# Input projection of a Mamba-2 layer in pairs of tiles: seven half-size products instead of eight

## The chip, the core and the metric

The kernel runs on one core of a Trainium2 chip. The core has five engines with an instruction queue each: TensorE (PE, matrix products, with its weight loads shown as PEld), VectorE (DVE, element-wise work), ScalarE (ACT, element-wise functions), GpSimd (POOL) and SyncE (SP), which here issues the DMA transfers. An engine works through its own queue in order and waits on semaphores for the others. [...] The metric is the device time of one execution in microseconds.

## What is computed

One layer (DEPTH is 1): RMSNorm, an input projection, a causal convolution, a state-space scan, a gate, RMSNorm, an output projection, the residual, and a last RMSNorm. x is 512 tokens of 2048 features.

```python
def ssm_mixer(h, w_in, conv_w, conv_b, dt_bias, a_log, d_skip, norm_g, w_out):
    proj = h @ w_in                                  # (512, 2048) @ (2048, 10304)
    z = proj[..., :D_INNER]                          # 4096
    xbc = proj[..., D_INNER:D_INNER + CONV_DIM]      # 4096 of x, 1024 of B, 1024 of C
    dt = proj[..., D_INNER + CONV_DIM:]              # 64
    xbc = jax.nn.silu(causal_depthwise_conv(xbc, conv_w, conv_b)).astype(jnp.float32)
    ...
    y = ssd_chunked_scan(xs * dt[..., None], dt * a, bm, cm)
    y = y + d_skip.astype(jnp.float32).reshape(g, r, 1) * xs
    y = y.reshape(bsz, length, D_INNER) * jax.nn.silu(z.astype(jnp.float32))
    y = rmsnorm(y, norm_g)
    return y.astype(h.dtype) @ w_out
```

All is f32. The product `h @ w_in` is 80 column tiles of 128 (32 of x, 32 of z, 8 of B, 8 of C) and dt.

## The kernel before

**Products in three terms.** TensorE works on the type fp32r. Each operand is split into a high part (ScalarE's cast, L80) and a low part (VectorE's subtraction, L81), and a product is hi·hi + hi·lo + lo·hi: three matmuls (`mm_k`, L177 to L179). A weight *piece* is half a column tile, 128x1024 f32 (eight blocks of 128 features). `load_piece` (L74) fetches it on SP's queue, `split_piece` splits it; the buffers `raw` (2) and `hi`, `lo` (3 each) go round. The normalised x lies split in `xh`, `xl`, one 128x512 tile for each of the 16 blocks of features.

**Order.** `seq` lists 80 column tiles: B0, C0, then for each unit u the tiles x_u and z_u; ahead of each second unit of a group of four stand the next group's B and C. A tile is 16 steps (blocks of features) of three matmuls with 512 columns into one PSUM tile `mm`, 48 matmuls in all. At its end `finish` hands it to `conv_silu` (x, B, C: scaling into `xr`, L361, four convolution steps L363 and L366, Silu L368) or to `u_z` (gate).

**State-space work.** A unit is two heads. Its steps hang on step numbers in a table `ev`: `u_load` fetches rows of decay exponents (`csb`, `ecs`), `u_decay` makes the masked decay matrix `m` (L436 to L444) with the group's `cbm` (L409), `u_xt` transposes x (L456), `u_state` (L477), `u_yd` (L489, L493), `u_yo` (L380 to L382, L511 to L520), which stores y to DRAM. TensorE and SP run in the order in which the program is written; VectorE and ScalarE are ordered by the framework's scheduler when the kernel is built, and keep that order on the chip.

**Behind it** come the output projection (`mm_o`, L629 to L631, from 1002.8 us on) and the last norm. The change leaves their arithmetic alone.

Of the kernel before, what the change touches and what calls it, by code (L numbers as in the profile page):

```python
# [28 lines left out]
EPS = 1e-6  # L29


@with_exitstack
def mamba_layer(ctx: ExitStack, tc: tile.TileContext, d: dict, out: bass.AP):
# [7 lines left out]
    yp0 = ctx.enter_context(tc.tile_pool(name="yp0", bufs=1))  # L41
# [30 lines left out]
    def load_piece(src, shape):  # L72
        raw = wp.tile(shape, F32, name="raw", bufs=2)
        nc.sync.dma_start(raw, src)  # L74
        return raw

    def split_piece(raw, shape, pool):
        hi = pool.tile(shape, F32R, name="hi")
        lo = pool.tile(shape, F32R, name="lo")
        S.copy(out=hi, in_=raw)  # L80
        V.tensor_tensor(out=lo, in0=raw, in1=hi, op=ALU.subtract)  # L81
        return hi, lo
# [35 lines left out]
    NP = 2 * len(seq)  # L118
    pieces = {}

    def w_src(n):
        kind, i = seq[n // 2]
        return d["wi"][tile_of[kind] + i, :, (n % 2) * 8:(n % 2) * 8 + 8, :]

    def get_piece(n):
        if n in pieces or n >= NP + len(wo_order):
            return
        if n < NP:
            pieces[n] = split_piece(load_piece(w_src(n), WSH), WSH, wp)
        else:  # L130
            p, s = wo_order[n - NP]
            pieces[n] = split_piece(load_piece(wo_src(p, s), OSH), OSH, op if n % 4 == 3 else wp)


    xh = [xp.tile([P, L], F32R, name=f"xh{k}") for k in range(KT)]
    xl = [xp.tile([P, L], F32R, name=f"xl{k}") for k in range(KT)]
    xr = sp.tile([P, L + 3], F32, name="xr")

    xbuf = [("csb", 2), ("csb", 2), ("m", 2), ("msh", 1), ("msl", 1)]

    def load_x(k2):
        name, bufs = xbuf[k2 % 5]
        raw = sp.tile([P, 2, L], F32, name=name, bufs=bufs)
        n = 2 if k2 else 1
        for j in range(0, 2, n):
            nc.sync.dma_start(raw[:, j:j + n, :], d["xT"][:, 2 * k2 + j:2 * k2 + j + n, :])
        return raw

    def split_x(k2, raw):
        for j in range(2):  # L150
            k = 2 * k2 + j
            S.activation(xh[k], raw[:, j, :], AF.Identity, scale=lng[:, k:k + 1])
            V.scalar_tensor_tensor(out=xl[k], in0=raw[:, j, :], scalar=lng[:, k:k + 1],
                                   in1=xh[k].bitcast(F32), op0=ALU.mult, op1=ALU.subtract)
# [20 lines left out]
    def mm_k(ps, w, k8, k):  # L175
        hi, lo = w
        T.matmul(ps, hi[:, k8, :], xh[k], start=k == 0, stop=False)  # L177
        T.matmul(ps, hi[:, k8, :], xl[k], start=False, stop=False)  # L178
        T.matmul(ps, lo[:, k8, :], xh[k], start=False, stop=k == KT - 1)  # L179
# [28 lines left out]
    for k in range(KT):  # L208
# [35 lines left out]
        for t in range(2):  # L244
            mm_k(ps_bc[:, t, :], w0[t, k // 8], k % 8, k)
# [6 lines left out]
    for i in (0, 2):  # L252
# [81 lines left out]
    def dt_sums():  # L334
# [5 lines left out]
        V.tensor_tensor(out=nwl, in0=cs, in1=pl, op=ALU.subtract)  # L340
        V.tensor_tensor(out=win[:, 0, :], in0=nwl[:, 0, :], in1=pl[:, 1, :], op=ALU.subtract)
        V.tensor_copy(out=win[:, 1, :], in_=nwl[:, 1, :])
        S.activation(win, win, AF.Exp, scale=-1.0)

    def dt_spread():
# [3 lines left out]
        cst = sp.tile([H, NC, P], F32, name="xd", bufs=2)  # L349
# [9 lines left out]
    def conv_silu(ps, t, name, bufs):  # L359

        V.tensor_tensor(out=xr[:, 3:L + 3], in0=ps, in1=rbc, op=ALU.mult)  # L361
        ca = sp.tile([P, L], F32, name=name, bufs=bufs)
# [7 lines left out]

    def split(src, shape, name, bufs=1):
# [6 lines left out]
    def mm3(o, a, b, sa, sb):  # L378

        T.matmul(o, a[0][sa], b[0][sb], start=True, stop=False)  # L380
# [31 lines left out]
    def u_load(u):  # L412
        csb = sp.tile([P, 2, L], F32, name="csb", bufs=2)
# [6 lines left out]
    def u_decay(u):  # L420
# [3 lines left out]
        m = sp.tile([P, 2, 6 * P], F32, name="m", bufs=2)  # L424
        ma = m[:, :, 0:4 * P].rearrange("p c (h l) -> p c h l", h=2)
        mb = m[:, :, 4 * P:6 * P].rearrange("p c (h l) -> p c h l", h=2)
        for i in range(2):
            for hh in range(2):
# [3 lines left out]
                for o, l, b in ((ma[:, i, hh, 0:P], la, cs[:, 2 * i, h:h + 1]),  # L432
                                (ma[:, i, hh, P:2 * P], lb, nwl[:, 2 * i, h:h + 1]),
                                (mb[:, i, hh, :], lb, cs[:, 2 * i + 1, h:h + 1])):
                    if i == 0:
                        S.activation(o, l, AF.Relu, scale=-1.0, bias=b)  # L436
                    else:
# [320 lines left out]
```

## Time and profile before

| | |
|---|---|
| median of 3 runs | 1374.59 us (1374.23 to 1374.94) |
| profiled execution | 1374.24 us, of which the span of the trace is 1372.5 |
| granted TensorE clock, mean | 0.997 |
| TensorE busy, 0 to 115 us / 115 to 1002.8 / behind | 107.4 / 887.8 / 360.5 us |
| VectorE busy in these stretches | 89.3 / 568.3 / 219.0 us |
| ScalarE busy in these stretches | 71.0 / 442.2 / 113.5 us |

A row of the trace's timeline has the start in us, the length in us, the engine, the line of the kernel, the operation, what it writes and reads, the shapes, and in brackets how long the engine had stood idle and who ended that. A row of the groups ends with busy time and mean length in ns, then the idle time before and its releasers. A row of the stretches has the stretch, its length, and the busy time and number of instructions of each engine, the granted clock, the share of the DMA engines and GB/s. In a row of the chain, engines stand with their share of the span.

### The profile page before, as it was taken

The numbers are of one execution on the slowest core, as the hardware profiler recorded it, in microseconds if no ns is written. First come the engines' busy times: TensorE is split into PE (matmuls) and PEld (weight loads), VectorE is DVE, ScalarE is ACT, GpSimd is POOL, SyncE is SP. The second block draws the span as 40 slices with busy tenths as digits, with TensorE's granted clock in tenths as the row PEclk, the third lists the DMA queues.
The fourth block names the chain that finished last, engine by engine and source line by source line (L and its number), as shares of the span: only waits on it lengthen the run. The fifth ranks groups of instructions, "written<-read, shape, count | busy, mean of one in ns | idle before, by whom it ended". The sixth has DMA issues, their size and how long they took to land.

```text
span 1372.5 us, 16466 instructions
## 1 busy us (share of the span) xinstructions
PE 1355.7 (99%) x6388; PEld 1097.1 (80%) x6388; DVE 876.7 (64%) x1433; ACT 626.6 (46%) x894; POOL 1.7 (0%) x11
## 2 busy tenths in 40 slices
PE   7999999999999999999999999999999999999997
PEld 5888878888888888888878888888888888888885
DVE  7867665765666575666557665667647665566545
ACT  7455653635465273546346443736453222223213
POOL 0000000000000000000000000000000000000000
PEclk9999999999999999999999999999999999999998
DMA  7333443523433252434324343424444445454402
GB/s 235 94 113 104 146 126 98 160 58 131 130 112 115 77 158 87 150 100 133 107 77 161 97 134 102 147 92 131 128 146 145 146 152 169 146 163 147 137 30 93
DMA packets 55182, 170.85 MB, mean 124 GB/s; under 512 B 6720, under 2 KB 11136, under 8 KB 54976
## 3 DMA queue, kind: packets, MB, share of 16 engines
q1 hardware_dynamic: 54384, 167.95, 38.4%
q10 hardware_dynamic: 720, 1.84, 0.4%
q8 instruction: 50, 0.82, 0.2%
q14 instruction: 28, 0.23, 0.1%
HBM read 156.99 MB, written 12.78 MB: 124 GB/s over the span
## 4 chain that ended last, share of the span: by engine, by line
PE 97%; DMA 1%; DVE 0%; SPq 0%; ACT 0%; issue 0%; DVEq 0%; ACTq 0%
PE mm L177 21%; PE mm L179 21%; PE mm L178 21%; PE mm L630 9%; PE mm L629 9%; PE mm L631 9%; PE yd L489 2%; DMA raw<-in_wi 1%; PE yd L493 1%; PE tr L456 1%; PE st L477 1%; PE yo L381 0%; PE yo L380 0%; PE yo L382 0%; PE tr L299 0%; PE tr L381 0%
## 5 line engine op out<-in xcount | busy, mean ns | idle before, releaser
L177 PE MATMUL mm<-xh,hi 128*128 128x512 f32 x1248 | 497.1, 398 | 0.0
L179 PE MATMUL mm<-xh,lo 128*128 128x512 f32 x1248 | 489.0, 392 | 0.0
L178 PE MATMUL mm<-xl,hi 128*128 128x512 f32 x1248 | 488.6, 392 | 0.0
L81 DVE TENSOR_TENSOR lo<-raw,hi 128x1024 fp32r<-128x1024 f32 x212 | 258.8, 1221 | 151.8 <-ACT hi L80 151.6
L80 ACT CAST hi<-raw 128x1024 fp32r<-128x1024 f32 x212 | 220.9, 1045 | 262.9 <-PE mm L178 108.6
L179 PEld LDWEIGHTS mm<-xh,lo 128*128 128x128 f32 x1248 | 234.4, 188 | 52.5
L177 PEld LDWEIGHTS mm<-xh,hi 128*128 128x128 f32 x1248 | 234.6, 188 | 51.7 <-issue 5.3
L178 PEld LDWEIGHTS mm<-xl,hi 128*128 128x128 f32 x1248 | 234.7, 188 | 46.2
L630 PE MATMUL mm<-lo,yh 128*128 128x512 f32 x512 | 201.9, 394 | 0.0
L629 PE MATMUL mm<-hi,yh 128*128 128x512 f32 x512 | 201.7, 394 | 0.0
L631 PE MATMUL mm<-hi,yl 128*128 128x512 f32 x512 | 201.7, 394 | 0.0
L629 PEld LDWEIGHTS mm<-hi,yh 128*128 128x128 f32 x512 | 96.2, 188 | 23.2 <-ACT acc L682 0.6
L631 PEld LDWEIGHTS mm<-hi,yl 128*128 128x128 f32 x512 | 96.1, 188 | 22.4
L630 PEld LDWEIGHTS mm<-lo,yh 128*128 128x128 f32 x512 | 96.1, 188 | 22.2
L519 ACT ACTIVATE z<-y 128x512 f32<-128x512 f32 x31 | 19.6, 633 | 123.5 <-DVE y L513 123.5
L686 DVE SCALAR_TENSOR_TENSOR acc<-mm,ry,acc 128x512 f32<-128x512 f32 x72 | 53.4, 747 | 30.5 <-PE mm L631 29.6
L366 DVE SCALAR_TENSOR_TENSOR xs<-xr,par,xs 128x512 f32<-128x512 f32 x96 | 71.8, 748 | 1.4
L436 ACT ACTIVATE m<-csb,cs 128x128 f32<-128x128 f32 x128 | 47.1, 391 | 51.4 <-DMA csb<-cscr 38.1
L442 DVE TENSOR_TENSOR m<-m,cbm 128x512 f32<-128x512 f32 x64 | 44.1, 689 | 38.5 <-ACT m L439 24.2
L368 ACT ACTIVATE xs<-xs 128x512 f32<-128x512 f32 x32 | 20.2, 632 | 69.2 <-DVE xs L366 69.2
L438 DVE TENSOR_SCALAR m<-csb,cs 128x128 f32<-128x128 f32 x128 | 33.7, 280 | 24.5 <-DMA csb<-cscr 24.4
L458 DVE TENSOR_TENSOR xd<-tr,dt 128x512 f32<-128x512 f32 x32 | 22.0, 687 | 31.3 <-PE tr L456 31.3
(211 smaller groups left out, 1173.2 us busy)
## 6 DMA issues: line engine op xcount, KB each, us to landing
raw<-in_wi SPq DMA_DIRECT2D x158, 512.0 KB, 3.9
raw<-in_wo SPq DMA_DIRECT2D x64, 512.0 KB, 4.1
csb<-cscr SPq DMA_DIRECT2D x32, 512.0 KB, 5.8
yscr<-y SPq DMA_DIRECT2D x32, 256.0 KB, 2.3
yr<-yscr SPq DMA_DIRECT2D x16, 512.0 KB, 4.7
ecs<-escr SPq DMA_DIRECT2D x64, 64.0 KB, 5.4
xt<-in_x SPq DMA_DIRECT2D x16, 256.0 KB, 4.6
csb<-in_xT SPq DMA_DIRECT2D x3, 512.0 KB, 8.9
```

Of the source, the lines that this page charges most:

```text
L80: S.copy(out=hi, in_=raw)
L81: V.tensor_tensor(out=lo, in0=raw, in1=hi, op=ALU.subtract)
L177: T.matmul(ps, hi[:, k8, :], xh[k], start=k == 0, stop=False)
L178: T.matmul(ps, hi[:, k8, :], xl[k], start=False, stop=False)
L179: T.matmul(ps, lo[:, k8, :], xh[k], start=False, stop=k == KT - 1)
L366: V.scalar_tensor_tensor(out=ca, in0=xr[:, k:k + L], scalar=convw[:, t, k:k + 1], in1=ca, op0=ALU.mult, op1=ALU.add)
L436: S.activation(o, l, AF.Relu, scale=-1.0, bias=b)
L442: V.tensor_tensor(out=ma[:, i], in0=ma[:, i], op=ALU.mult, in1=cbm[:, i, 0:2, :].rearrange("p b l -> p (b l)").unsqueeze(1).to_broadcast([ ...
L629: T.matmul(ps, yh, hi, start=k == 0, stop=False)
L630: T.matmul(ps, yh, lo, start=False, stop=False)
L631: T.matmul(ps, yl, hi, start=False, stop=k == n - 1)
L686: V.scalar_tensor_tensor(out=a, in0=ps, scalar=ry[:, t:t + 1], in1=a, op0=ALU.mult, op1=ALU.add)
```

## The change

The first four pairs of tiles (B0 C0, x0 z0, x1 z1, B1 C1: `plain`) are computed as before. The other 36 pairs (`quads`) are computed by a scheme of seven products of half size. Call the pair's first tile (x or B) p and its second (z or C) q. The features are cut in two halves, the tokens too. The four weight pieces of a pair are R11 and R12 (p's two halves of features) and R21, R22 (q's), and sums of them serve as operands too:

- T1 = R11 + R12, T2 = T1 + R22, T3 = R12 + R22, T4 = T2 + R21: four sums by VectorE, in place (`q_add`, L561), each then split like a piece: seven splits a pair.
- The other operands are halves of x and sums of them (`x_forms`, in `form`, and `x_form3`, which overwrites a quarter of `xh`, `xl`), made once and kept on chip.
- Each product is 8 blocks x 3 matmuls of 256 columns. They run in the order R11, T4 *of the pair before*, T1, R21, T2, R22, T3. R11, T2 and T3 add up in one half of a PSUM tile S (even pairs the one half, odd pairs the other), T1 and R22 in R; R21 and T4 in the `mm` tile of p. ScalarE copies S into that `mm` tile after R11 and after T3 (L603, L615), S and R into `sn` after T2 and T1 (L610, L607); VectorE adds them up to q (L612, L614).
- 28 steps (of six matmuls) a pair in the step table instead of 32 of three.

Beside it: the split products of B with C and of the state become f32 products (L408, L409, L462); the decay is made by ScalarE alone with one VectorE product of 128x1536 (L436); `csb`, `m` and `xd` have one buffer instead of two; R11's split has a buffer of its own, `h1h`, `h1l`; units' steps come later (`ramp` and the six numbers behind it); the wider PSUM for the output projection opens 1.5 blocks later.

```diff
-MANUAL = {mybir.EngineType.PE, mybir.EngineType.SP}
+MANUAL = {mybir.EngineType.PE, mybir.EngineType.SP, mybir.EngineType.Pool}
...
+    plain = [s for pair in (seq[0], seq[1], seq[2], seq[3]) for s in pair]
+    quads = seq[NPL // 2:]
+    QS = 28
...
+    def x_forms(g, j):
+        k = 4 * g + 2 * j
...
+        V.tensor_tensor(out=t1, in0=n2[:, :, hi_], in1=n1[:, :, hi_], op=ALU.subtract)
+        V.scalar_tensor_tensor(out=t2, in0=t1, scalar=-1.0, in1=n1[:, :, lo_], op0=ALU.mult, op1=ALU.subtract)
+        put(1, t1)
+        V.scalar_tensor_tensor(out=t1, in0=t2, scalar=-1.0, in1=n2[:, :, lo_], op0=ALU.mult, op1=ALU.subtract)
+        put(2, t2)
+        put(4, t1)
...
+    def q_add(n, f, old, other):
+        raw = qs[n][old]
+        V.tensor_tensor(out=raw, in0=raw, in1=qs[n][other], op=ALU.add)
+        qs[n][f] = raw
...
+    def q_events(n):
+        b = NPL * KT + n * QS
+        for o, f, a in ((-34, q_load, ("R11", 0, 0, "ra")), (-9, q_split, ("R11", True)),
+                        (-7, q_load, ("R12", 0, 1, "rb")), (-1, q_add, ("T1", "R11", "R12")),
+                        (0, q_split, ("T1",)), (-5, q_load, ("R21", 1, 0, "rc")), (2, q_split, ("R21",)),
+                        (-4, q_load, ("R22", 1, 1, "rc")), (10, q_add, ("T2", "T1", "R22")),
+                        (11, q_split, ("T2",)), (16, q_split, ("R22",)), (17, q_add, ("T3", "R12", "R22")),
+                        (18, q_split, ("T3",)), (21, q_add, ("T4", "T2", "R21")), (22, q_split, ("T4",))):
+            add(b + o, f, n, *a)
...
+    def product(ps, w, f, first, step):
+        for k in range(KH):
+            if k % 2 == 0:
+                run(step + k // 2)
+            hi, lo = w()
+            ah, al = operand(f, k)
+            T.matmul(ps, hi[:, k, :], ah, start=first and k == 0, stop=False, skip_group_check=True)
+            T.matmul(ps, hi[:, k, :], al, start=False, stop=False, skip_group_check=True)
+            T.matmul(ps, lo[:, k, :], ah, start=False, stop=k == KH - 1, skip_group_check=True)
+
+    def pair(n, prev):
...
+        s_, r_ = [x[:, (n % 2) * LH:(n % 2) * LH + LH] for x in SR]
...
+        product(s_, W("R11"), 11, True, b)
+        S.copy(out=A[:, lo_], in_=s_)
+        if prev:
+            prev(b + 4)
+        product(r_, W("T1"), 1, True, b + 8)
+        S.copy(out=sn[:, 1, :], in_=r_)
+        product(A[:, lo_], W("R21"), 12, False, b + 12)
+        product(s_, W("T2"), 2, False, b + 16)
+        S.copy(out=sn[:, 0, :], in_=s_)
+        product(r_, W("R22"), 4, False, b + 20)
+        V.tensor_tensor(out=zq[:, lo_], in0=r_, in1=sn[:, 0, :], op=ALU.add)
+        product(s_, W("T3"), 3, False, b + 24)
+        V.tensor_tensor(out=zq[:, hi_], in0=s_, in1=sn[:, 1, :], op=ALU.add)
+        S.copy(out=A[:, hi_], in_=s_)
...
+        def last(step):
+            product(A[:, hi_], W("T4"), 22, False, step)
+            normed(A)
+            (g_b if kp == "B" else u_x)(ip)
...
+        w = ramp[u] if u < len(ramp) else [24, 38, 50, 58, 61, 66]
+        for o, f in zip(w, (u_load, u_decay, u_xt, u_state, u_yd, u_yo)):
+            add(at["x", u] + o, f, u)
...
+    for i in range(4):
+        add(49 + 7 * i, x_forms, i // 2, i % 2)
+        add(120 + 2 * i, x_form3, i)
```

**What moves on VectorE, in the middle of the run.** Before, VectorE's queue from the scaling of a finished x tile (`xr`) on; the weight piece that is split between (`lo<-raw`) is one that TensorE needs two pieces later.

```order
L361 TENSOR_TENSOR xr<-mm,rbc 128x512 [waits DVE_49,PE_49]
L438 TENSOR_SCALAR m<-csb,nwl 128x128
L363 TENSOR_SCALAR xs<-xr,par 128x512 [waits DVE_49]
L81 TENSOR_TENSOR lo<-raw,hi 128x1024 [waits DMAHW0_49,Activation_49]
L366 SCALAR_TENSOR_TENSOR xs<-xr,par,xs 128x512 [waits DVE_49]
L438 TENSOR_SCALAR m<-csb,cs 128x128
```

Now, in the third pair of a group: T3's sum (`rb<-rb,rc`), `xr` when T4 of the pair before is done, the convolution with the steps behind `yo` between, `m`, the running sum of squares, and then T2's low part (`lo<-ra,hi`).

```order
L561 TENSOR_TENSOR rb<-rb,rc 128x1024
L374 TENSOR_TENSOR xr<-mm,rbc 128x512 [waits PE_49]
L365 TENSOR_SCALAR xs<-xr,par 128x512 [waits DVE_49]
L492 TENSOR_TENSOR ecs<-yo,ecs 128x256 [waits DMAHW6_49,DMAHW5_49,PE_49]
L368 SCALAR_TENSOR_TENSOR xs<-xr,par,xs 128x512 [waits DVE_49]
L493 TENSOR_TENSOR y<-y,ecs 128x256 [waits DVE_49]
L368 SCALAR_TENSOR_TENSOR xs<-xr,par,xs 128x512 [waits DVE_49]
L494 TENSOR_TENSOR y<-y,z 128x512 [waits DVE_49]
L368 SCALAR_TENSOR_TENSOR xs<-xr,par,xs 128x512 [waits DVE_49]
L436 TENSOR_TENSOR m<-m,cbm 128x1536 [waits Activation_49]
L500 TENSOR_TENSOR sx<-sx,z 128x512 [waits Activation_49]
L82 TENSOR_TENSOR lo<-ra,hi 128x1024
```

T2 is the third product behind T4 on TensorE, so its split stands behind work that begins only with T4's end. In the same place T1, R22 and T3 stand ahead of or behind this run of rows.

**What moves on TensorE where one piece of work follows another.** Before, the last matmuls of one column tile and the first of the next: they write different PSUM tiles (`mm_3755`, `mm_3869`) and wait for nothing.

```order
L178 MATMUL mm_3755<-xl15_137,hi_3707 128x512
L179 MATMUL mm_3755<-xh15_121,lo_3708 128x512
L177 MATMUL mm_3869<-xh0_106,hi_3751 128x512
L178 MATMUL mm_3869<-xl0_122,hi_3751 128x512
L179 MATMUL mm_3869<-xh0_106,lo_3752 128x512
```

Now, the last matmuls of T3 and the first of the next pair's R11, both into S:

```order
L590 MATMUL S<-xl,hi 128x256
L591 MATMUL S<-xh,lo 128x256
L589 MATMUL S<-xh,h1h 128x256 [waits Activation_49]
L590 MATMUL S<-xl,h1h 128x256
L591 MATMUL S<-xh,h1l 128x256
```

The wait is new. The count that it waits for is that of ScalarE's copy of S into `mm` (L615), which stands on ScalarE's queue thus, and itself waits for VectorE's read of S (L614):

```order
L610 COPY sn<-S 128x256 [waits PE_49]
L81 CAST hi<-ra 128x1024 [waits DVE_49,PE_49,Activation_49]
L615 COPY mm<-S 128x256 [waits DVE_49]
L621 ACTIVATE z<-z 128x512 [waits DVE_49]
L81 CAST hi<-rc 128x1024 [waits DMAHW3_49,PE_49,Activation_49]
```

What moved: a read of PSUM that ran beside the next tile's matmuls now stands between two products of TensorE.

More of the change, by code (lines that the diff above doesn't have):

```diff
@@ L286, in dt_load @@
     def dt_load():
-        wd = load_piece(d["wdt"], [P, KT, HD])
-        wa = [sp.tile([P, KT // 2, P], F32R, name=n) for n in ("msh", "msl")]
+        wd = load_piece(d["wdt"], [P, KT, HD], "rb")
+        wa = [sp.tile([P, KT // 2, P], F32R, name=n) for n in ("csb", "m")]
         for i in range(2):
@@ L369, in conv_silu, with normed @@
         return ca
+    def normed(ps):
+        V.tensor_tensor(out=xr[:, 3:L + 3], in0=ps, in1=rbc, op=ALU.mult)
     def split(src, shape, name, bufs=1):
@@ L518, in u_yo, with put @@
         else:
-            S.activation(sq, y, AF.Square)
-            V.tensor_tensor(out=sx, in0=sx, in1=sq, op=ALU.add)
+            S.activation(z, y, AF.Square)
+            V.tensor_tensor(out=sx, in0=sx, in1=z, op=ALU.add)
+    lo_, hi_ = slice(0, LH), slice(LH, L)
+    form = {}
+    def x_forms(g, j):
+        k = 4 * g + 2 * j
+        n1, n2 = [(sp if n in ("csb", "m") else wp).tile([P, 2, L], F32, name=n, bufs=1)
+                  for n in (("csb", "m"), ("h1h", "h1l"))[j]]
+        for n, k0 in ((n1, k), (n2, KH + k)):
+            nc.sync.dma_start(n, d["xT"][:, k0:k0 + 2, :])
+            for i in range(2):
+                S.activation(n[:, i, :], n[:, i, :], AF.Identity, scale=lng[:, k0 + i:k0 + i + 1])
+        if j == 0:
+            for f, s in ((1, 0), (2, 4), (4, 8)):
+                form[f, g] = [xp.tile(SSH, F32R, name=f"s{s + 2 * g + i}") for i in range(2)]
+        jj = slice(2 * j, 2 * j + 2)
+        t = wp.tile([P, 2, 2, LH], F32, name="rc", bufs=2)
+        t1, t2 = t[:, 0], t[:, 1]
+        def put(f, t):
+            hi, lo = [x[:, jj, :] for x in form[f, g]]
+            S.copy(out=hi, in_=t)
+            V.tensor_tensor(out=lo, in0=t, in1=hi, op=ALU.subtract)
+        V.tensor_tensor(out=t1, in0=n2[:, :, hi_], in1=n1[:, :, hi_], op=ALU.subtract)
[4 more added lines that the diff above has]
+        put(4, t1)
@@ new lines, in x_form3, with q_split @@
+    def x_form3(j):
+        kk = slice(2 * j, 2 * j + 2)
+        h, lo = xh[:, kk, hi_], xl[:, kk, hi_]
+        t = sp.tile([P, 2, LH], F32, name="y", bufs=2)
+        V.tensor_tensor(out=t, in0=xh[:, kk, lo_], in1=h, op=ALU.subtract)
+        V.tensor_tensor(out=t, in0=t, in1=xl[:, kk, lo_], op=ALU.add)
+        V.tensor_tensor(out=t, in0=t, in1=lo, op=ALU.subtract)
+        S.copy(out=h, in_=t)
+        V.tensor_tensor(out=lo, in0=t, in1=h, op=ALU.subtract)
+    def q_split(n, f, own=False):
+        raw = qs[n][f]
+        qs[n, f] = split_piece(raw, WSH, wp, *((("h1h", "h1l"), 1) if own else ()))
@@ L598, in mamba_layer @@
     add(b0 + 56, dt_spread)
-    for n in range(2, len(seq)):
+    for n in range(2, NPL):
         ps = None
@@ L614, in mamba_layer @@
             finish(n, ps)
+    prev = None
+    SR = [ps_q.tile([P, L], F32, name=x) for x in ("S", "R")]
+    for n in range(len(quads)):
+        prev = pair(n, prev)
+    prev(END)
     phx.close()
-    assert NP + 3 not in pieces
     op = ctx.enter_context(tc.tile_pool(name="op", bufs=1, side="right"))
     acc = [op.tile([P, DM], F32, name=f"acc{t}") for t in range(NC)]
-    step = len(seq) * KT
+    step = END + 4
     def mm_o(ps, blk, w, t):
```

302 lines of the change are left out of this document (151 added, 151 removed).

## The prediction

> **What bounds the kernel now.** I read the page's totals first, then its chain of work, then the busy time of the engines over the stretch that the change rewrites. That stretch runs from the end of the eighth column tile (115 us) to the first matmul of the output projection (1002.8 us).
>
> ```profile
> span 1372.5 us, 16466 instructions
> PE 1355.7 (99%) x6388; PEld 1097.1 (80%) x6388; DVE 876.7 (64%) x1433; ACT 626.6 (46%) x894; POOL 1.7 (0%) x11
> PE 97%; DMA 1%; DVE 0%; SPq 0%; ACT 0%; issue 0%; DVEq 0%; ACTq 0%
> 115.00:1002.80 887.80, 887.80 (x4333) 720.25 (x4332) 568.31 (x968) 442.15 (x628) 0.00 (x0) 1.00 0.37 116
> ```
>
> The reader is to see that TensorE (PE) has no idle time at all in these 887.8 us, that VectorE (DVE) is busy for 64% of them and ScalarE (ACT) for half. The 36 pairs of tiles take 887.8/36 = 24.66 us each: 96 matmuls and the state-space work between them. VectorE waits, never TensorE.
>
> **Durations that the sum uses.** On TensorE the listed length of a matmul holds its latency, so I take distances between starts: two rows twelve matmuls apart for 512 columns, and a burst of six with 256 columns, each with weights of its own (the only such burst), up to the matmul behind it.
>
> ```profile
> 399.66 0.39 PE L177 MATMUL mm<-xh,hi 128*128 128x512 f32 x1
> 402.40 0.39 PE L177 MATMUL mm<-xh,hi 128*128 128x512 f32 x1
> ```
> ```profile
> 1006.95 0.28 PE L477 MATMUL st<-xwsh,bth 128*128 128x256 f32 x1
> 1006.95 0.19 PEld L477 LDWEIGHTS st<-xwsl,bth 128*128 128x128 f32 x1
> 1007.54 0.28 PE L477 MATMUL st<-xwsh,btl 128*128 128x256 f32 x1
> 1007.66 0.39 PE L629 MATMUL mm<-hi,yh 128*128 128x512 f32 x1
> ```
>
> 512 columns: 2.74/12 = 0.228 us. 256 columns: 0.71/6 = 0.118 us, a little over half. The listed 0.19 us of a weight load overlap the matmul ahead, so it sets no pace in the burst. After a wait it is seen:
>
> ```profile
> 14.63 1.41 DVE L153 SCALAR_TENSOR_TENSOR xl<-m,lng,xh 128x512 fp32r<-128x512 f32 x2
> 15.44 0.50 PE L178 MATMUL yd<-xl,hi 128*128 128x512 f32 x1 [0.63 <-DVE xl L153]
> 15.78 0.40 PE L179 MATMUL yd<-xh,lo 128*128 128x512 f32 x1
> ```
>
> The first of these two operations of VectorE ends at 15.38 and TensorE starts 0.06 us later; its matmul takes 0.34 instead of 0.23 up to the next. A wait thus costs 0.06 + 0.11 = 0.17 us more.
>
> ```profile
> 638.45 0.65 PE L489 MATMUL yd<-m,xd 128*64 128x256 f32 x4
> 639.90 0.51 PE L177 MATMUL mm<-xh,hi 128*128 128x512 f32 x1
> ```
> ```profile
> L336 PE MATMUL tr<-y,mask 128*128 128x256 f32 x2 | 0.6, 378 | 0.0
> L380 PE MATMUL yo<-csth,stsh 128*128 128x256 f32 x32 | 9.0, 280 | 0.0
> ```
>
> The matmuls of one unit's `yd` occupy 1.45 us. A full-width f32 pass of 256 columns is listed 98 ns longer than the 256-column form above, so it streams for 118 + 98 = 216 ns. The new f32 state (two matmuls, each of two passes over 128 columns) is then about 0.45 us, the new f32 `cbm` products 4 x 0.216 + 4 x 0.108 = 1.3 us a group. These two are estimates. A unit's four transposes I set at 0.5 us, its three `yo` matmuls at 0.35.
>
> ```profile
> 612.72 1.22 DVE L81 TENSOR_TENSOR lo<-raw,hi 128x1024 fp32r<-128x1024 f32 x1
> 613.85 0.74 DVE L366 SCALAR_TENSOR_TENSOR bc<-xr,par,bc 128x512 f32<-128x512 f32 x1
> 614.51 1.22 DVE L81 TENSOR_TENSOR lo<-raw,hi 128x1024 fp32r<-128x1024 f32 x1
> 616.31 0.42 DVE L444 TENSOR_TENSOR m<-m,cbm 128x256 f32<-128x256 f32 x1
> 616.65 0.68 DVE L442 TENSOR_TENSOR m<-m,cbm 128x512 f32<-128x512 f32 x1
> 622.47 0.69 DVE L361 TENSOR_TENSOR xr<-mm,rbc 128x512 f32<-128x512 f32 x1
> 623.07 0.28 DVE L438 TENSOR_SCALAR m<-csb,nwl 128x128 f32<-128x128 f32 x1
> 623.26 0.54 DVE L363 TENSOR_SCALAR xs<-xr,par 128x512 f32<-128x512 f32 x1
> 623.72 1.22 DVE L81 TENSOR_TENSOR lo<-raw,hi 128x1024 fp32r<-128x1024 f32 x1
> ```
> ```profile
> 48.29 0.69 DVE L361 TENSOR_TENSOR xr<-yd,rbc 128x512 f32<-128x512 f32 x1
> 49.02 0.55 DVE L363 TENSOR_SCALAR bc<-xr,par 128x512 f32<-128x512 f32 x1
> ```
>
> VectorE back to back: 1.13 us for 128x1024 of two tensors, 0.60 for 512, 0.34 for 256, 0.66 for the three-operand form of 512, 0.46 for the one-tensor form. This is a base of 0.07 us and 1.04 ns an element, so the new `m` product of 1536 is 1.67. A result that the next instruction needs costs 0.13 more (0.73 instead of 0.60).
>
> ```profile
> L80 ACT CAST hi<-raw 128x1024 fp32r<-128x1024 f32 x212 | 220.9, 1045 | 262.9 <-PE mm L178 108.6 <-PE mm L631 92.8 <-DMA raw<-in_wi 34.6
> L374 ACT CAST stsh<-st 128x256 fp32r<-128x256 f32 x16 | 5.9, 371 | 50.0 <-PE st L477 50.0
> ```
> ```profile
> 607.38 0.40 ACT L436 ACTIVATE m<-csb,cs 128x128 f32<-128x128 f32 x1 [0.46 <-DMA csb<-cscr]
> 607.69 0.39 ACT L436 ACTIVATE m<-csb,nwl 128x128 f32<-128x128 f32 x1
> 609.27 1.28 ACT L439 ACT_TABLE_LOAD   x1
> ```
> ```profile
> 605.60 1.05 ACT L80 CAST hi<-raw 128x1024 fp32r<-128x1024 f32 x1 [0.46 <-DMA raw<-in_wi]
> 606.68 1.23 DVE L81 TENSOR_TENSOR lo<-raw,hi 128x1024 fp32r<-128x1024 f32 x1 [0.82 <-ACT hi L80]
> ```
> ```profile
> 77.77 0.39 PE L177 MATMUL mm<-xh,hi 128*128 128x512 f32 x1
> 77.97 0.69 DVE L361 TENSOR_TENSOR xr<-mm,rbc 128x512 f32<-128x512 f32 x1 [1.92 <-PE mm L179]
> ```
>
> ScalarE casts 128x1024 in 1.05 us and copies 256 columns out of PSUM in 0.37; a decay step of 128 takes 0.31, a change of its function table 1.28. From ScalarE's end to VectorE's start pass 0.03 us, and from the moment TensorE is free for its next matmul to the reader of its result 0.20.
>
> **The change, part by part.** *Matmuls:* 96 x 0.228 = 21.9 us a pair become 168 x 0.118 = 19.9. With 2.75 us of unit work a pair would take 22.6 us if TensorE never waited, 2 us less than now. *VectorE:* seven splits 7.9 us and four sums 4.5 (now four splits, 4.5), sums out of PSUM 0.7, z, xr and xd 1.8, convolution 2.4, `m` 1.67, xw and the state's split 0.5, y 0.66, the chain behind `yo` 1.9: 22.1 us a unit pair. It fits under 22.6 only if it is never late.
>
> *The loop.* It is late, because of two orders shown above. First, the product R11 of a pair writes the same PSUM tile S from which the last product of the pair before (T3) is still to be read, and TensorE waits there for ScalarE's copy, which itself waits for VectorE's read. Second, T2's low part stands on VectorE behind the whole convolution of the x tile, which can only begin when T4 is done. Followed from the end of one T3 (time 0) to the end of the next:
> - read of S at 0.20, 0.42 us; 0.03; copy 0.37; 0.17: R11 starts at **1.2**.
> - R11 24 x 0.118 = 2.84 and the state 0.45: done 4.5. T4 and `yd`, 2.84 + 1.5, end at 8.8.
> - `h1h` has one buffer: the cast of the next R11 waits for R11's end, 0.20 + 1.05 + 0.03, so VectorE begins its low part at 5.8. Behind it stand T2's sum, y and T3's sum: 1.13 + 1.13 + 0.66 + 1.13. VectorE reaches `xr` at **9.8**, so T4's end is no longer what it waits for.
> - `xr` 0.60, dependent 0.13, 0.46, ecs 0.34, three of 0.66, 0.34, 0.60, `m` 1.67, sum of squares 0.60, T2's low part 1.22: 7.9. It is ready at **17.8**. TensorE reached T2 at 1.2 + 4 x 2.84 + 0.45 + 1.5 + 0.35 = 14.9 and waits for some 2.6 us behind two matmuls that need only the high part.
> - from there 0.17, 22 x 0.118 = 2.6 to T2's end, R22 with transposes 3.34, T3 2.84, in all 8.95: **26.7**.
>
> Against 24.66 that is 2.0 us more. The five pairs of a group differ: the first (unit 4g) has the `cbm` products too, 28.0. In the second the sum of squares stands behind T2's low part, but ScalarE's cast for R21 stands ahead of the copy of S and delays R11 by about 1 us: `xr` at 2.2 + 7.7 + 0.2 = 10.1, then 7.3 and 8.95, 26.4. The third (B and C) 26.7. In the fourth T2's low part stands directly behind `xr`, so that only the wait for the copy is left: 1.2 + 19.9 + 2.5 = 23.6. In the fifth VectorE comes 0.9 us late to S and ScalarE begins the decay only at 7.5, after two casts that wait for R11; it takes 12 x 0.31 + 1.28 + 0.95 = 5.9. At 13.4 follow `m`, a convolution step and T2's low part, 1.67 + 0.66 + 1.22: 16.95, and 8.95 behind it make 25.9. Together **130.6** against 123.3. All 36: 23.6 + 25.9, six groups, then 28.0 + 26.4 + 2 x 26.7 = 940.9, so +53.1.
>
> No row of before shows a wait of TensorE for a copy out of its own tile. It lies between 0, if copy and product overlapped, and 1.2 us; I take 1.2, because the built order holds the wait. [...]
>
> *The ramp.* The sums of x need 4 x 3.72 + 4 x 2.4 = 24.5 us on VectorE before the first pairs, the first split and sum 2.3 more.
>
> ```profile
> 25.00:115.00 90.00, 89.79 (x425) 73.64 (x425) 72.83 (x135) 52.20 (x81) 0.00 (x0) 1.00 0.39 123
> ```
>
> Between 25 and 115 us VectorE was idle for 90 - 72.8 = 17.2 us. Splits and decay work that go, some 1.5 us a unit and 0.6 a tile of B, give back about 5 (an estimate). So 26.8 - 5 - 17.2 = 4.6 us do not fit at the least, and 26.8 at the most. I take **9**, near the lower end, since VectorE cannot use all its idle time in a fixed order.
>
> *The rest:* output projection 0 (its two PSUM buffers last some 8 groups longer: up to +3). DMA moves the same weights plus 4 MB of x, 0 while it comes in time.
>
> The profiled execution took 1374.24 us around its span of 1372.5, 0.35 below the median of the runs. Sum: 1374.2 + 53.1 + 9 = **1436**.
>
> **Rivals.**
> - *The read of S costs nothing* (the wait overlaps the weight loads): 1436 - 36 x 1.2 = 1393. Against it stands the wait in the order.
> - *Weights come late.* The load for R11 of the pair after next waits until T4 is split and stands on SP's queue ahead of R21 and R22. Two MB then start within 2 us. If T2's sum waits 2 us in each pair: 1436 + 72 = 1508. For it: that order. Against it: DMA engines are 37% busy.
> - *TensorE stays the bound* (the other side). This holds if the way from R11's end through cast, `h1l`, sums, convolution and T2's low part takes no more than T4, T1 and R21, 10.4 us; I have 13.3. Then 36 x 19.9 + 32 x 2.75 + 9.3 = 814 us, so 1374 - 74 + 9 = 1309. For it: VectorE's 22.1 of 22.6 us.
> - *A shorter loop cancels out* (sums or conv 2 us cheaper): about 1370.
> - *Weight loads set the pace*, 0.188 us each: 168 x 0.188 = 31.6 us a pair, 1374 + 36 x 9.7 + 9 = 1732. Against it: six loads in 0.71 us. [...]
>
> **Chances.** Forecast 0.58 (by itself 1410 to 1465); S free 0.14; weights late 0.10; TensorE bound 0.10; cancelled 0.05; weight loads 0.03. A measurement tells 0.2% (2.7 us) from no change. Faster: 0.10 and 0.02 of the cancelled case; same 0.03; slower 0.85. The range 1375 to 1495 takes in forecast, S free and the nearer half of late weights.
>
> **What would show it.** From the first `cbm` of one group to that of the next some 130 us (123.3 now). TensorE idle before each R11, ended by the copy of S, and before T2's first low-part matmul, ended by VectorE's split, 36 and about 28 times. Matmuls of 256 columns 0.118 us apart. `xr` not waiting for TensorE. Wrong: a gap before R11 under 0.5 us, `xr` ending a wait for T4, or idle time before R21 and R22 ended by DMA.

## The result and the profile after

The changed kernel takes **1526.51 us** (median of 4 runs, 1525.76 to 1528.91) against 1374.72 us before: 1.111 times as long, interval [1.109, 1.113]. Slower was forecast, at 1436 us with a range up to 1495; the time lies 31 us above that range. The profiled execution took 1526.35 us.

The page's totals, its clock row and its chain, as for the kernel before:

```profile
span 1524.6 us, 22159 instructions
PE 1347.7 (88%) x8980; PEld 1221.7 (80%) x8980; DVE 1137.6 (75%) x1477; ACT 785.2 (52%) x1291; POOL 1.8 (0%) x11
PEclk9998999999999999999999999999999999999999
PE 49%; DVE 25%; DMA 11%; ACT 7%; issue 6%; SPq 1%; ACTq 0%; DVEq 0%
```

TensorE held 97% of the chain before and holds 49% now: the rest belongs to engines that it waits for. The busy time by stage (ramp, the 36 pairs, output projection; PE, PEld, DVE, ACT and POOL, then the granted clock, the DMA share and GB/s) says where:

```profile
25.00:124.77 99.77, 90.88 (x421) 73.81 (x420) 78.84 (x131) 62.61 (x103) 0.00 (x0) 0.97 0.38 124
124.77:1145.31 1020.54, 874.67 (x6921) 840.98 (x6919) 817.29 (x1010) 581.31 (x985) 0.00 (x0) 0.94 0.31 103
1145.31:1524.60 379.29, 363.42 (x1576) 292.52 (x1574) 222.87 (x309) 120.47 (x169) 0.00 (x0) 0.99 0.40 132
```

| stretch | before | forecast | after |
|---|---|---|---|
| up to the first pair | 115.0 | +9 | 124.8, +9.8 |
| 36 pairs | 887.8 | +53.1 | 1020.5, +132.7 |
| output projection | 369.7 | 0 | 379.3, +9.6 |

The miss is in the pairs, about 80 us of it, and in the output, 10. In the pairs TensorE, idle for nothing before, now stands still before R11 and inside T2. The waits in total (waiting engine, operation and line, what for: us, times, longest):

```profile
PE S L591 <- DVE lo L82: 67.0, 29, 4.7
PE S L589 <- ACT mm L615: 65.1, 35, 4.0
PE S L589 <- ACT hi L81: 3.7, 6, 0.7
PE R L591 <- DVE lo L82: 3.3, 1, 3.3
```

One group of five pairs in the timeline, only the rows behind a wait (start, duration, instruction, idle time and releaser):

```profile
574.39 0.39 PE L589 MATMUL S<-xh,h1h 128*128 128x256 f32 x1 [3.93 <-ACT mm L615]
588.11 0.38 PE L589 MATMUL S<-s,hi 128*128 128x256 f32 x1 [0.60 <-ACT hi L81]
590.77 0.39 PE L591 MATMUL S<-s,lo 128*128 128x256 f32 x1 [2.16 <-DVE lo L82]
600.63 0.38 PE L589 MATMUL S<-xh,h1h 128*128 128x256 f32 x1 [0.90 <-ACT mm L615]
618.09 0.39 PE L591 MATMUL S<-s,lo 128*128 128x256 f32 x1 [3.21 <-DVE lo L82]
630.66 0.39 PE L589 MATMUL S<-xh,h1h 128*128 128x256 f32 x1 [2.36 <-ACT mm L615]
646.24 0.39 PE L591 MATMUL S<-s,lo 128*128 128x256 f32 x1 [1.32 <-DVE lo L82]
657.57 0.58 PE L589 MATMUL S<-xh,h1h 128*128 128x256 f32 x1 [2.49 <-ACT mm L615]
675.55 0.38 PE L591 MATMUL S<-s,lo 128*128 128x256 f32 x1 [2.61 <-DVE lo L82]
685.25 0.39 PE L589 MATMUL S<-xh,h1h 128*128 128x256 f32 x1 [0.90 <-ACT mm L615]
711.86 0.58 PE L589 MATMUL S<-xh,h1h 128*128 128x256 f32 x1 [3.88 <-ACT mm L615]
725.58 0.39 PE L589 MATMUL S<-s,hi 128*128 128x256 f32 x1 [0.61 <-ACT hi L81]
728.24 0.38 PE L591 MATMUL S<-s,lo 128*128 128x256 f32 x1 [2.15 <-DVE lo L82]
739.47 0.39 PE L589 MATMUL S<-xh,h1h 128*128 128x256 f32 x1 [0.90 <-ACT mm L615]
```

R11 of the pair with the `cbm` products starts at 600.63, the next ones at 630.66, 657.57, 685.25, 711.86 and 739.47: 30.0, 26.9, 27.7, 26.6 and 27.6 us, 138.8 a group where 130.6 were forecast.

**The clock.** Some rows behind a wait are listed at 0.58 us instead of 0.39. The stretch around 657.57, cut where the granted clock changes:

```profile
655.20:657.20 2.00, 0.00 (x0) 0.00 (x0) 1.92 (x3) 1.00 (x2) 0.00 (x0) 1.00 0.93 342
657.20:660.60 3.40, 3.03 (x14) 3.03 (x15) 1.22 (x1) 1.46 (x4) 0.00 (x0) 0.51 0.93 329
660.60:662.60 2.00, 2.00 (x19) 2.00 (x19) 1.43 (x2) 0.90 (x3) 0.00 (x0) 0.98 0.17 66
```

TensorE stops at 655.1; two microseconds later the granted clock falls to half and stays there for 3.4 us, in which matmuls of 256 columns start 0.213 us apart instead of 0.118. The distances above 0.118 add up to **49.9 us** over the 36 pairs; this is called the half-clock excess below. A wait alone doesn't decide it: the 3.21 us at 618.09 were followed by full speed, the 2.49 at 657.57 were not. The trace's record of the granted clock shows what does. All 30 falls in it, from 80.4 to 1159.0 us, lie on one raster with a step of 3.413 us. In the pairs the clock fell behind every step at full clock of which TensorE had been idle for 1.99 us or more (25 steps); of those with 1.75 to 1.93 idle microseconds it fell behind three and not behind four, and behind none with less. The wait before 618.09 lies across the end of a step at 616.30, 1.4 us on one side and 1.8 on the other.

Behind 21 of the 28 falls in the pairs the half clock lasted one step, 3.41 us, behind the other seven two, 6.83. The fall at 814.3, for one, lies 157.0 us or 46.0 steps behind the one at 657.3.

So 1020.5 us split into 145.9 idle, 49.9 of half-clock excess, and 824.7 of work. The record of the granted clock gives a check on the excess: in the pairs it stands at a half for 119.5 us, and TensorE is busy for 110 of them. If half of these are lost, that is 55 (an estimate; by the distances, 0.213 us for 0.118, it is 49). The excess is thus known to some 5 us here. The same split for the forecast of 940.9: the matmuls and unit work that it lists make 36 x 19.9 + 32 x 2.75 + 9.3 = 813.7, so its waits were 127.2, and it had nothing for the clock.

### The profile page after: what moved, and what is told of

It is laid out like the page before. It is cut to its first block, busy times and chain, and to the rows that moved or that the text cites. A ratio compares the mean times of both kernels' runs of the same rounds, so it can differ in the third digit from the quotient of the medians.

```text
span 1524.6 us, 22159 instructions
## 1 busy us (share of the span) xinstructions
PE 1347.7 (88%) x8980; PEld 1221.7 (80%) x8980; DVE 1137.6 (75%) x1477; ACT 785.2 (52%) x1291; POOL 1.8 (0%) x11
## 4 chain that ended last, share of the span: by engine, by line
PE 49%; DVE 25%; DMA 11%; ACT 7%; issue 6%; SPq 1%; ACTq 0%; DVEq 0%
DVE lo L82 7%; PE mm L748 7%; PE mm L749 7%; PE mm L747 7%; DMA rc<-in_wi 6%; PE S L589 4%; PE S L591 4%; PE S L590 4%; ACT hi L81 4%; DVE xs L368 3%; DMA rb<-in_wi 2%; DVE ra L561 2%; PE mm L589 2%; DVE m L436 2%; PE mm L591 1%
## 5 line engine op out<-in xcount | busy, mean ns | idle before, releaser
L81 ACT CAST hi<-ra 128x1024 fp32r<-128x1024 f32 x168 | 175.8, 1047 | 282.5 <-DVE ra L561 145.8
L82 DVE TENSOR_TENSOR lo<-ra,hi 128x1024 fp32r<-128x1024 f32 x168 | 205.0, 1220 | 80.8 <-ACT hi L81 79.5
L589 PE MATMUL mm<-xh,hi 128*128 128x256 f32 x576 | 165.5, 287 | 2.6 <-ACT mm L615 2.6
L591 PE MATMUL mm<-xh,lo 128*128 128x256 f32 x576 | 162.4, 282 | 4.1 <-DVE lo L82 4.1
L589 PE MATMUL R<-s,hi 128*128 128x256 f32 x576 | 165.9, 288 | 0.0
L591 PE MATMUL R<-s,lo 128*128 128x256 f32 x576 | 162.8, 283 | 3.3 <-DVE lo L82 3.3
L590 PE MATMUL R<-s,hi 128*128 128x256 f32 x576 | 162.6, 282 | 0.0
L590 PE MATMUL mm<-xl,hi 128*128 128x256 f32 x576 | 162.3, 282 | 0.0
L589 PE MATMUL S<-xh,h1h 128*128 128x256 f32 x288 | 94.4, 328 | 65.1 <-ACT mm L615 65.1
L589 PEld LDWEIGHTS mm<-xh,hi 128*128 128x128 f32 x576 | 109.8, 191 | 7.6 <-issue 4.8
L589 PEld LDWEIGHTS R<-s,hi 128*128 128x128 f32 x576 | 111.2, 193 | 0.0
L590 PEld LDWEIGHTS R<-s,hi 128*128 128x128 f32 x576 | 110.7, 192 | 0.0
L590 PEld LDWEIGHTS mm<-xl,hi 128*128 128x128 f32 x576 | 109.7, 190 | 0.0
```

Of the source, the lines that this page charges most:

```text
L589: T.matmul(ps, hi[:, k, :], ah, start=first and k == 0, stop=False, skip_group_check=True)
L590: T.matmul(ps, hi[:, k, :], al, start=False, stop=False, skip_group_check=True)
L591: T.matmul(ps, lo[:, k, :], ah, start=False, stop=k == KH - 1, skip_group_check=True)
```

## The experiments

Three theories. **A**: TensorE's waits at R11 and T2 are two separate faults, one of tiles and one of VectorE's order, and each can be taken away for its own price. **B**: VectorE's queue sets the pair, by its load and by what it waits for; TensorE's waits only show the slack. **C**: the half-clock stretches are part of the price. The split of the pairs for each run that bears on them, worked out as above, is that of the profiled execution; the time is the median of all:

| run | time | ratio to before | pairs | idle | half-clock excess |
|---|---|---|---|---|---|
| the change | 1526.5 | 1.111 [1.109, 1.113] | 1020.5 | 145.9 | 49.9 |
| e1: S and R swapped | 1495.5 | 1.088 [1.086, 1.090] | 991.8 | 119.7 | 56.5 |
| e2: T2 early | 1458.8 | 1.062 [1.059, 1.065] | 949.9 | 105.3 | 21.0 |
| e3: both | 1458.4 | 1.062 [1.060, 1.063] | 953.7 | 91.4 | 32.2 |
| e5: no sums | 1462.9 | 1.065 [1.062, 1.067] | 960.4 | 109.4 | 28.5 |
| e8: both, no sums | 1374.4 | 1.000 [0.999, 1.002] | 869.3 | 44.0 | 10.4 |
| e11: 8 fillers | 1513.0 | 1.101 [1.100, 1.103] | 1005.4 | 113.8 | 37.4 |

By the check with the granted clock the last column is known to some 7 us; in e8 it is too high, for its pairs have half the clock for only 17.1 us, 14.6 of them busy, which makes 7.3.

One thing is in all these prices. For every build the scheduler orders the queues of VectorE and ScalarE anew. Against the change, at least 139 of VectorE's 1477 instructions stand elsewhere in its queue in e1, 236 in e2 and 344 in e3; in e11 none does. An edit's price holds the order that came with it.

### S and R swapped in every second pair

```diff
-        s_, r_ = [x[:, (n % 2) * LH:(n % 2) * LH + LH] for x in SR]
+        s_, r_ = [x[:, (n % 2) * LH:(n % 2) * LH + LH] for x in (SR if n % 2 == 0 else SR[::-1])]
```

> Every second pair swaps the tiles S and R, so that R11 no longer writes the tile that T3 has just left. Theory A (TensorE's two waits, plus the half clock that follows them, are the loss): the 65 us of idle time before R11, ended by the copy of S, fall under 15 us, the waits before T2 stay near 67 us, and the time falls by 50 to 85 us, to 1440 to 1476. Theory B (VectorE's own chain of work sets the length of a pair, and TensorE's waits are only where the slack shows): the idle time moves from R11 to T2 or R21, and the time stays within 1510 to 1530.

1495.5 us, 31 less, between the two. The waits for the copy of S (L615) before R11 are gone from the list; the waits in T2, for its low part and for its cast, grew from 70.7 to 109.0 (the first two rows below hold 3.5 us before T1 too):

```profile
PE R L591 <- DVE lo L82: 49.3, 19, 4.2
PE S L591 <- DVE lo L82: 46.8, 17, 4.6
PE S L589 <- ACT hi L81: 9.2, 3, 3.2
PE R L589 <- ACT hi L81: 7.2, 4, 2.3
```

The wait was real, as the forecast had it, and the tile was its cause. But TensorE came to T2 earlier and VectorE hardly did: 38 of the 65 us turned up there.

### T2's sum and split handed out four steps earlier

```diff
-                        (-4, q_load, ("R22", 1, 1, "rc")), (10, q_add, ("T2", "T1", "R22")),
-                        (11, q_split, ("T2",)), (16, q_split, ("R22",)), (17, q_add, ("T3", "R12", "R22")),
+                        (-4, q_load, ("R22", 1, 1, "rc")), (6 if n else 10, q_add, ("T2", "T1", "R22")),
+                        (7 if n else 11, q_split, ("T2",)), (16, q_split, ("R22",)), (17, q_add, ("T3", "R12", "R22")),
```

> T2's sum and split are handed out four steps earlier, so that T2's low part stands ahead of most of the convolution on VectorE; products and tiles stay. Theory A: the 67 us of idle time within T2, ended by VectorE's split, fall under 20 us and with them part of the half-clock time; the 65 us before R11 stay; 1440 to 1475. Theory B: the convolution, m and the later splits end no earlier, the idle time moves to R22, T3 or R11, and the time stays within 1510 to 1530.

1458.8 us, 68 less, as A has it. The waits in T2 are gone, and the half-clock excess fell by 29 us; a new wait of 31.1 us stands before R22's low part (the second row also holds 3.3 before T1, which the change has too):

```profile
PE S L589 <- ACT mm L615: 63.4, 35, 4.7
PE R L591 <- DVE lo L82: 34.5, 29, 3.3
```

### Both edits

> Both edits at once: S and R swapped in every second pair, and T2's sum and split handed out early. Swapping alone gave -31 us, early T2 alone -68. Theory A (two separate waits of TensorE): the gains add, 1420 to 1435, and no wait over 10 us in all is left before R11 or T2. Theory B (VectorE's queue, busy 22.7 us a pair and idle some 5 behind casts, sets the length once TensorE is on time): the gains overlap, 1440 to 1458, and the idle time stands before R22 or T3, ended by VectorE's splits, 60 us or more.

1458.4 us: the swap, worth 31 us alone, is worth nothing here. That is B, at the edge of what it stated. Nearly all waits for the copy are gone, and VectorE's splits end 77.7 us of waits in S and R instead, 65.4 of them in R22 and T3:

```profile
PE R L591 <- DVE lo L82: 38.9, 28, 3.4
PE S L591 <- DVE lo L82: 38.8, 31, 2.1
DVE lo L82 <- ACT hi L81: 102.7, 104, 4.9
```

The busy time over the pairs:

```profile
124.79:1078.47 953.68, 862.30 (x6920) 826.26 (x6918) 815.46 (x1010) 585.84 (x985) 0.00 (x0) 0.96 0.34 110
```

VectorE is busy for 815.5 of 953.7 us, 86%, and for much of the rest it stands in its one queue behind a cast of ScalarE (102.7 us in 104 waits, over the whole span). But the chain that ended last has more in it than VectorE:

```profile
PE 34%; DVE 30%; DMA 18%; ACT 11%; issue 4%; SPq 1%; DVEq 0%; ACTq 0%
```

10% of the span are loads of `csb`, which has one buffer since the change, some 8 us each, and 6% are loads into `rc`. No run gave `csb` its second buffer back, so what this part of the change costs by itself is open.

### The sums left out, alone and with both edits

```diff
         raw = qs[n][old]
-        V.tensor_tensor(out=raw, in0=raw, in1=qs[n][other], op=ALU.add)
         qs[n][f] = raw
```

> The four weight sums of each pair are left out (T1, T2, T3 and T4 then use plain weights, so the output isn't the layer's); VectorE has 18.1 us of work a pair instead of 22.7, TensorE the same. Theory B (VectorE's load): T2's low part comes two sums (2.3 us) earlier, its 67 us of waits fall under 15, ScalarE's casts no longer wait for sums, and the time falls by 90 us or more, under 1436. Theory A (order of tiles and queues, not load): R11's 65 us stay, T2's fall by less than half, 1470 or more.

> Tiles swapped, T2 early, and the four weight sums left out (T1, T2, T3 and T4 use plain weights, so the output isn't the layer's). Either set alone gave -68 and -64 us. Theory B (with TensorE's own waits gone VectorE's queue sets the pair: 26.5 us at some 23.4 of work): 4.5 us less of work let TensorE set it, 23 to 24.5 us a pair, 1335 to 1390. Rival (the casts, which wait for free buffers and late weights, set the pair whatever VectorE does): 1420 to 1458.

Alone 1462.9 us, between the two statements: R11's waits stay at 52 us and T2's at 43, which is nearer to A. VectorE has 146 us less to do and the pairs lose 60. With both edits the same omission takes 84 us off 1458.4 and lands at 1374.4, within B's 1335 to 1390. TensorE is then idle for 44.0 us in the 36 pairs:

```profile
124.94:994.25 869.31, 825.28 (x6920) 796.53 (x6919) 658.76 (x866) 574.01 (x984) 0.00 (x0) 0.99 0.37 121
```

So leaving out the sums saves 84 us once TensorE's order is mended, and 64 with its waits there. This is more than VectorE's work alone: with both edits ScalarE's casts waited 109 us for sums (51.0 for those in `ra`, 58.3 in `rb`), and these waits go too. Even with sums for nothing, and with TensorE's order mended, the kernel only draws level: the pairs gain 18.5 us on the 887.8 of before, and ramp and output give them back.

### The sums on GpSimd, or by transfers

```diff
-        V.tensor_tensor(out=raw, in0=raw, in1=qs[n][other], op=ALU.add)
+        Q.tensor_tensor(out=raw, in0=raw, in1=qs[n][other], op=ALU.add)
```

> The four weight sums of a pair go from VectorE to GpSimd; VectorE is relieved of 4.5 us of 22.7 a pair. No row shows a sum on GpSimd. Theory B (VectorE's chain sets the pair): T2's low part comes some 2.3 us sooner, its 67 us of waits fall under 20, and the time falls by 60 to 110 us, to 1415 to 1465, if GpSimd takes under 3 us for one. Theory A alone (tile order and queue order, not load): the R11 waits stay at 60 us or more and the time falls by less than 60. If a sum takes over 4 us on GpSimd, or slows VectorE, T1 and T2 wait for it instead: 1530 or more.

1671.4 us (ratio 1.216 [1.214, 1.219]), 145 more, though a sum took GpSimd only 2.4 to 3.0 us on average, by its operands. The cast of T1's sum stands on ScalarE ahead of the copy of S, and the sum is now late: R11's waits rose from 65 to 180 us. And a split on VectorE that began while GpSimd worked took 3.09 us instead of 1.22:

```profile
242.64 2.79 POOL L561 TENSOR_TENSOR ra<-ra,rc 128x1024 f32<-128x1024 f32 x1 [11.86 <-DVE lo L82]
243.43 3.09 DVE L82 TENSOR_TENSOR lo<-rc,hi 128x1024 fp32r<-128x1024 f32 x1 [0.26 <-ACT hi L81]
```

The sum ends at 245.43 and the split 1.09 us later, which is about its whole usual time. Over the span VectorE is listed busy for 1085.7 us, where 144 sums less of 1.22 us would have left 962: some 0.86 us of VectorE's time are lost for each sum on GpSimd. What holds VectorE up there no row shows.

With both edits and only the sums for T3 and T4 on GpSimd:

> As both edits at once, and the sums for T3 and T4, which have half a pair of slack, go to GpSimd, where a sum took 2.36 us in the run with all four. VectorE has 20.4 us a pair. Theory B: 30 to 70 us below the run with both edits, since VectorE's queue is what sets the pair; with 1380 or less the change would break even. Theory A: within 15 us of the run with both edits. If GpSimd makes VectorE slower or T3 waits for its sum (rb has one buffer, so R12's next load starts later): above the run with both edits.

1516.8 us (1.106 [1.102, 1.109]), 58 above the run with both edits: the last of the three statements. T3's sum frees `rb` later, so T1's sum is late (it waits 17.8 us for the load of `rb`, 2.5 with both edits alone; ScalarE's casts wait 252.7 us for sums in `ra`, 51.0 with both edits alone).

With the sums as accumulating transfers started by GpSimd, `nc.gpsimd.dma_start(raw, w_half(...), accum_op=ALU.add)` in place of the addition, and T1's, T3's and T4's handed out 7 steps earlier:

> As with both edits, and each sum is made by an accumulating transfer from the weights in memory, started by GpSimd, instead of VectorE; four more transfers of 512 KB a pair, in place of VectorE's 4.5 us. No row shows such a transfer. Theory B: if one lands within 5 us, the time comes within 20 us of the run without the sums. If it takes 8 us or more, T1 and T2 wait for it (the chain in ra holds three sums one after another): 1480 or more.

1444.1 us (1.050 [1.048, 1.053]): neither. A transfer landed 8.2 us (`ra`) or 11.0 us (`rb`) after its issue, and the DMA engines were 78% busy in the pairs. The output of this run isn't the layer's, for a reason that stays open, so its time stands for transfers of this size and order only.

### Fillers for the waits

32 useless matmuls a pair, 12 before R11 and 20 before T2, into the `yd` tile that is free there:

```diff
+    def warm(count, w):
+        dm = ps_yd.tile([P, 2, 2 * P], F32, name="yd")
+        for k in range(count):
+            T.matmul(dm[:, 0, :], w()[0][:, k % KH, :], xh[:, k % KH, lo_], start=True, stop=True, skip_group_check=True)
...
+        warm(12, W("R11"))
         product(s_, W("R11"), 11, True, b)
...
+        warm(20, W("T2"))
         product(s_, W("T2"), 2, False, b + 16)
```

> 32 useless matmuls of 256 columns a pair are added into the yd tile, 12 ahead of R11 and 20 ahead of T2, where TensorE waits now; they take 3.8 us a pair at full clock, 136 us in all. Theory C (the stretches after the waits at half the granted clock cost some 45 us of the time): the granted clock over the pairs rises from 0.94 to 0.98 or more, and the time falls to 1485 to 1515 though work is added; some 25 us are given back where the waits were shorter than the filling. Rival (the slow stretches are taken up by waits that follow anyway): 1526 to 1560, the clock higher and the waits longer.

1568.4 us (1.141 [1.139, 1.143]): 42 more, above both statements. The half-clock excess halved, to 24.3, but the fillers made TensorE late at T2 where the wait had been shorter, and they moved the order in which VectorE's work was queued. This run tells nothing of C. Eight fillers before R11 alone, with VectorE's queue as in the change, are the cleaner form (`warm(8, W("R11"))`, the second call left out):

> Eight useless matmuls of 256 columns (0.94 us) ahead of every R11, into the yd tile, where TensorE waits 0.9 us or more in any case; unlike the run with 32 of them, the order of VectorE's queue is the same as without them. Theory C (half-clock stretches lengthen the pair): the half-clock excess behind R11's waits, 18 us in 11 pairs now, falls under 8, and the time falls by 6 to 18 us, though work is added and none taken away. Rival (the next wait takes it up): the time changes by less than 4 us.

1513.0 us: **13.5 us less with 288 matmuls more**. The half-clock excess fell by 12.5 us, and the idle time by about what the fillers take (32.1 against 288 x 0.118 = 34.0). Behind R11's waits alone it fell less than stated, from 16.0 to 9.8 us in those products. The rest is in the products that follow, most of it in T2, where no filler stands; where the steps of the clock's raster fell may have a share in that.

The trace of the changed kernel says the same without any edit. The pairs that start at 574.39 and at 711.86 hold the same place in their group and the same waits, 0.60 + 2.16 + 0.90 and 0.61 + 2.15 + 0.90 us. Only the clock differs behind the wait in T2:

```profile
590.77:594.17 3.40, 3.40 (x28) 3.40 (x29) 3.35 (x3) 1.75 (x3) 0.00 (x0) 1.00 0.06 10
728.24:731.64 3.40, 3.40 (x18) 3.40 (x19) 3.35 (x3) 1.38 (x2) 0.00 (x0) 0.60 0.05 10
```

The first pair is 26.24 us long with 1.64 of excess, the second 27.61 with 2.94: 1.37 longer for 1.30 more. A line fitted through the last 30 distances from one R11 to the next, with a level of its own for each of the five places in a group, gives 0.9 to 1.1 us of length for each us of excess, by the way in which the excess is counted (standard error 0.2). Within this execution no later wait visibly takes the excess up.

Between executions of one kernel it is taken up in part. Over the 51 executions of the eleven kernels with the change in them, the time rose by 0.50 us (standard error 0.08) for each us by which (1 - granted clock) x time rose. With both edits it rose least: the profiled execution had a clock of 0.967, the other three 0.978 or 0.979, which is 16 us of lost clock, and it took 2.9 us more than their mean. C holds, then; the 49.9 us are what TensorE lost, and what the time would fall by without them lies between half of that and all of it.

## Why the prediction was wrong, step by step

- **Duration of 256 columns, 0.118 us:** right wherever the clock was full. TensorE's work in the pairs came to 815 to 830 us in the runs of the table (e11's fillers taken off) against the 813.7 listed; the rival in which weight loads set the pace at 0.188 is refuted.
- **The failed step: the sum of the loop has no term for the clock.** From "R11 starts at 1.2" to "26.7" every matmul is taken at 0.118 us, with the waits only added in. The waits themselves made TensorE run behind them at a granted clock of a half, with 0.213 us a matmul instead of 0.118: 49.9 us in 36 pairs. In the pairs of the kernel before, nothing shows the price, since TensorE never waited there. Its trace does show such a pace at one place on which the prediction doesn't draw, behind the first wait of all, where matmuls of 512 columns start 0.42 us apart before they fall to 0.23 (the record of the granted clock begins only at 10.3 us, at full clock, so these rows show the pace and not its cause):

```profile
8.78 0.63 PE L178 MATMUL yd<-xl,hi 128*128 128x512 f32 x1
9.21 0.63 PE L179 MATMUL yd<-xh,lo 128*128 128x512 f32 x1
9.63 0.63 PE L177 MATMUL yd<-xh,hi 128*128 128x512 f32 x1
...
10.64 0.39 PE L177 MATMUL yd<-xh,hi 128*128 128x512 f32 x1
10.87 0.40 PE L178 MATMUL yd<-xl,hi 128*128 128x512 f32 x1
```
- **R11 waits for the copy of S: right, but mis-sized.** 1.2 us a pair were taken, 43 in all; 65.1 were measured. The bare read costs 0.90 us. It is more where a cast stands on ScalarE ahead of the copy: at 657.57 the cast of T1's sum, which had waited through VectorE for the load of R12, and at 630.66 the cast of R21, which waited for its load:

```profile
629.29 1.04 ACT L81 CAST hi<-rc 128x1024 fp32r<-128x1024 f32 x1 [0.93 <-DMA rc<-in_wi]
630.25 0.37 ACT L615 COPY mm<-S 128x256 f32<-128x256 f32 x1
```
```profile
654.86 1.22 DVE L561 TENSOR_TENSOR ra<-ra,rb 128x1024 f32<-128x1024 f32 x1 [1.97 <-DMA rb<-in_wi]
656.20 1.04 ACT L81 CAST hi<-ra 128x1024 fp32r<-128x1024 f32 x1 [5.91 <-DVE ra L561]
657.15 0.37 ACT L615 COPY mm<-S 128x256 f32<-128x256 f32 x1
```

- **The rival of late weights** is thus true in part, at another place than it named: weights reach R11 through a cast that blocks the copy, and not T2's sum. How much of the time it explains is open: in the chain that ended last, loads into `rc` and `rb` stand for 8% of the span, where all transfers stood for 1% before, and no run gave these tiles another buffer.
- **T2 waits for VectorE: right.** "Some 2.6 us", about 28 times, make 73; 67.0 us in 29 waits were measured, and early T2 removed them.
- **The price of S by itself (the rival "S free", 36 x 1.2 = 43 us) was wrong as a way of reckoning.** With S free the time fell by 31 us alone and by nothing once T2 was early: the two waits share VectorE's chain and don't add.
- **The five pairs of a group:** 28.0, 26.4, 26.7, 23.6, 25.9 forecast; 30.0, 26.9, 27.7, 26.6, 27.6 measured. The largest miss is the fourth, which was given the bare wait alone and has 3.88 us before the next R11.
- **VectorE, 22.1 us a unit pair:** 817.3/36 = 22.7 measured, on average over all pairs.
- **`xr` doesn't wait for TensorE:** nearly right, 11.8 us in 9 waits in all.
- **Ramp +9:** measured +9.8. **Output 0, up to 3:** wrong, +9.6. Some 6.5 us are waits of TensorE, most of them for PSUM buffers of the first partial sums, whose copies stand on ScalarE behind the decay of the last unit (which is ScalarE's alone now); 1.6 us are half clock behind the longest, and the last 1.5 stay open:

```profile
1152.00 0.50 PE L747 MATMUL mm<-hi,h1h 128*128 128x512 f32 x1 [1.64 <-ACT acc L800]
1158.46 0.50 PE L747 MATMUL mm<-hi,h1h 128*128 128x512 f32 x1 [3.45 <-ACT acc L800]
1203.27 0.47 PE L747 MATMUL mm<-hi,yh 128*128 128x512 f32 x1 [0.30 <-issue]
1204.83 0.50 PE L748 MATMUL mm<-lo,yh 128*128 128x512 f32 x1 [1.09 <-DVE lo L82]
```

In sum, TensorE's time splits the 90 us between forecast and result thus: 50 are the clock, 19 longer waits (145.9 against 127.2), 11 work that the list of matmuls had left out or taken too short, 10 the output and 1 the ramp. By the check with the granted clock it is 55 of the clock and 6 of such work.

No run beats the kernel before. What was not tried: the order of VectorE and ScalarE written out by hand, and another buffer for `rb`, `rc` or `csb`.

## What to carry to other kernels

A transformation that saves an eighth of the matmuls pays only if what it adds fits under the engine that was the bound: here 4.5 us of sums a pair, on an engine already busy for two thirds, were worth 84 us even with TensorE's order mended. When a kernel that never let TensorE wait gets waits of 2 us and more, price the half-clock stretch behind them as well as the wait (49.9 us beside 145.9 idle here); where such a wait can't be avoided, useless matmuls in it can pay, as long as they end before the wait does (13.5 us less with eight a pair, 42 more with 32). And take waits out in combination before adding up their prices: two waits on one chain were worth 31 and 68 us apart, and 68 together.

## What the hardware showed unexpectedly

In the run of the change the granted clock fell at the end of a step of 3.413 us, on one raster for all 30 falls, when TensorE had been idle for about 2 us of that step (in the pairs always from 1.99 on, never below 1.75). Equal waits thus cost nothing, some 1.5 us of excess (one step at half clock) or some 2.5 (two), by where they lie on the raster. A sum of two 128x1024 tensors on GpSimd, 2.4 us and more, held up VectorE for 0.86 us on average, which leaves a relief of some 0.3 us (1.13 less 0.86).
